# Alternating the matmuls of two accumulators in a hybrid gMLP and pooling layer

## The chip, the core and the metric

The kernel runs on one core of one Trainium2 chip. A core has a matrix engine (TensorE, PE in the profile; its weight loads are PEld), a vector engine (VectorE, DVE), a scalar engine (ScalarE, ACT), GpSimd (POOL) and SyncE (SP), which issues most of the DMAs here. The engines run side by side, each through its own list of instructions in order, and wait for each other by semaphores. The metric is the device time of one execution in microseconds, the median of several runs.

## The reference

One layer of a streaming encoder is computed for 4096 new rows of a prompt and 32 rows of a sample stream, with model width 1024, all in float32:

- h = RMSNorm(x); one projection h @ w_in gives five parts of 1024 columns: u, v, z_a, x_b, z_b.
- Branch A: v is layer-normed; per head (8 heads of 128 columns) a masked 128x128 matrix mixes the 128 positions of a chunk; a = u * (mixed v + bias) * silu(z_a).
- Branch B: trailing means of x_b over 2, 4, 8 or 16 rows minus x_b itself, a linear map for each of four groups, a scale; b = that * silu(z_b).
- y = x + concat(a, b) @ w_out, then a final RMSNorm. Also returned are the last 15 rows of x_b for both streams and the normed v rows of the sample.

## The kernel before

*Products.* Every large matrix product is done in two ways at once. It is cut 2 x 2 and computed with seven block products instead of eight (the Strassen scheme in Winograd's form): operand sums are made beforehand, the seven products are numbered q = 0 to 6, and their results are added up. And each float32 operand is split into a high and a low part that TensorE takes in one pass each (type float32r); a product of two operands is high x high, high x low and low x high. So one block product over four slices k of 128 is twelve matmuls (lines 186 to 194, `product`): for each k the pairs (stationary, moving) are (high, high), (high, low), (low, high). All twelve add into one accumulator, a PSUM bank of 128 x 512 float32. TensorE is told at the first of them to overwrite, where the accumulator is a fresh one.

*Accumulators.* `Combine` (lines 146 to 179) names the accumulators of one output block and what happens behind each product. Products 0, 1, 3 and 5 begin a fresh bank. Products 2 and 4 go on adding to the bank of product 0, product 6 to that of product 3. Behind product 0, ScalarE copies bank 0 into y11 (line 167); behind product 1, VectorE adds bank 1 to y11 (line 165); behind product 2, ScalarE copies bank 0 again into y21 (line 172); behind product 4 it copies it into y12 (line 174) and VectorE adds bank 3 to make y22; behind 5 and 6 VectorE adds banks 5 and 3. So product 2 may not write bank 0 before the copy of line 167 has read it, product 4 not before that of line 172, product 6 not before the sum behind product 4. Six banks serve the pool `ps_acc2`, two more the spatial mixing.

*Stages.* From 0 to about 52 us x_b's and the pool's weights are multiplied together and operands are made; until about 400 us v is projected; from then to 1704 us runs the input projection for the gates, u and the pooling branch, the loop in question; the rest is the output projection (lines 712 to 714) with the final norm.

*The loop in question.* Tokens are four blocks of 1024 rows (b = 0 to 3). In each block there are 16 sets of weight columns: eight of kind gate (z_a and u for one head) and eight of kind pool. The order in a block is a pair of pool sets, eight gate sets one by one, four pool sets one by one, a pair of pool sets; the products of a pair are interleaved by `lagged` (line 181). A set's seven products use 128 weight columns of each half as the stationary operand and 512 token columns as the moving one. The last block also carries the 32 sample rows, so its token half is 528 wide and is worked in two column parts of 264 (`self.groups`), each with its own `Combine` and its own banks. Line 1156 begins a step (s, q): weight operands are prepared LEAD = 5 steps ahead (`prepare`, casts of line 119 on ScalarE and differences of line 81 on VectorE, into seven buffers of the pool `wop_p`); then the products of that step, each followed by its `after`; then, for a gate set, behind q = 2 and q = 4, the spatial mixing of one half (`spatial`, lines 993 to 1002: four float32 matmuls of 128 columns, which the profile shows as eight instructions of line 998, and one VectorE instruction). What finishes a set (silu, products, windows, stores) is traced in the first steps of the next.

*Order.* The program text gives an order of tracing, not the final order. A planner goes through the traced instructions with its own model of times: each engine gets the earliest traced instruction that is ready by that model, and the order found so is fixed in the program. Semaphore waits are then put where an instruction depends on another engine.

Of the kernel before, what the change touches and what calls it, by code (L numbers as in the profile page):

```python
# [36 lines left out]
def stream_step(ctx: ExitStack, tc, x_prompt, x_sample, state_pool, norm_g, w_in, ln_v_g, ln_v_b,  # L37
# [10 lines left out]
    mm = nc.tensor.matmul  # L48
# [15 lines left out]
    part = dram.tile([SEQ + DEC, D], F32, name="part")  # L64
# [121 lines left out]
    def product(comb_, q, stationary, moving, lo_last=False):  # L186

        acc, fresh = comb_.bank(q)
        terms = [(k, s, m) for k in range(4) for s, m in ((0, 0), (0, 1), (1, 0))]
        if lo_last:  # L190
            terms.sort(key=lambda x: x[1])
        for n, (k, s, m) in enumerate(terms):
            mm(acc, stationary(s, k), moving(m, k), start=fresh and n == 0, stop=n == len(terms) - 1,  # L193
               skip_group_check=True)

    def stacked(acc, rows, n, terms):

        last = len(terms) - 1
        for i, (st, wh, wl) in enumerate(terms):
            if i < last:  # L200
                mm(acc[:, :n], st, wh, start=i == 0, stop=False)
            mm(acc[:rows, :n], st[:, :rows], wl, start=False, stop=False)  # L202
        mm(acc[:, :n], st, wh, start=False, stop=True)

    def pool(name, bufs, stack=ctx, **kw):
        return stack.enter_context(tc.tile_pool(name=name, bufs=bufs, reuse_waits="tile", **kw))
# [4 lines left out]
    with ExitStack() as ph:  # L211
# [184 lines left out]
        def comb_rows(i):  # L396
            cols = []
            for q in range(2):
                tr = tr_tile()
                for cc in range(4):  # L400
                    c = 4 * q + cc
                    turn = nc.tensor.transpose(tr[:, cc * P:(cc + 1) * P], rows_t[i][:, c * P:(c + 1) * P], ident)
                    if i == 1 and c == 0:
                        tc.keep_in_program_order(turn)
                cols.append(half())
                (nc.scalar.copy if i > 1 else nc.vector.tensor_copy)(cols[q], tr)
            return cols
# [49 lines left out]
        class Pair:  # L457
# [72 lines left out]
            def product(self, q):  # L530
                t = self.ops[q].rearrange("p h (k t) -> p h k t", t=P)
                product(self.c, q, lambda h, k: t[:, h, k, :], lambda h, k: wv[q][:, h, k, :])
                self.c.after(q)
# [20 lines left out]
        parts = comb_rows(0)  # L554
        for i in range(KT):
# [8 lines left out]
            parts = nxt  # L564
# [56 lines left out]
    def raw_tile(dt=F32):  # L621
        return raw_p.tile([P, D], dt, tag="raw", name="raw")
# [9 lines left out]
    def load_out_weights(z, q):  # L632
        w_slots[z, q] = t = slot()[:, :4 * D].rearrange("p (k h n) -> p k h n", k=4, h=2)
        nc.sync.dma_start(t.bitcast(F32), wops[z, q].rearrange("p k (h n) -> p k h n", h=2))
# [229 lines left out]
    with ExitStack() as ph:  # L864
# [50 lines left out]
        class Tokens:  # L915
# [17 lines left out]
            def moving(self, q, h, k, c0, n):  # L933
                if self.last:
                    return self.ops[q].rearrange("p (h k t) -> p h k t", h=2, t=WIDE)[:, h, k, c0:c0 + n]
                return self.ops[q][:, :8 * HALF].rearrange("p (h j k t) -> p h k j t", h=2, j=4, t=P)[:, h, k]

        class Set:
# [40 lines left out]
            def combine(self, c0, n):  # L979
                def first(y):  # L980
                    if self.kind == "gate":
# [2 lines left out]
                return Combine(n, acc_tile, first,  # L984
                               *[lambda y=y: self.result(y, c0, n) for y in ("11", "12", "21", "22")])

            def product(self, c, q, c0, n):
                t = self.ops[q]
                product(c, q, lambda h, k: t[:, h, k, :], lambda h, k: self.tok.moving(q, h, k, c0, n),
                        self is groups[0][0] and q == 0)  # L990
                c.after(q)
# [117 lines left out]
        def prepare(upto):  # L1109

            nonlocal done
            while done < min(upto, len(steps)):
                while loads and loads[0][0] <= done + (AHEAD if done < first[id(groups[n_sets][0])] + 7 else 6):
                    loads.pop(0)[2].load()
                s, q = steps[done]
                s.prep[q]()
                if done in beside:
                    w, q = beside[done]
                    w.prep[q]()
                done += 1  # L1120
# [25 lines left out]
        for n in range(n_sets):  # L1146
            g, order = groups[n], orders[n]
            for s in g:
                s.begin()
            if n == n_sets - 5:  # L1150
                w_stack.close()
                spare_p = pool("spare_p", 2, side="right")
            elif n == n_sets - 1:
                groups[n_sets][0].begin([spare_p.tile([P, D], F32, tag="spare", name="spare") for _ in range(2)], True)
            cs = {id(s): [(s.combine(c0, w), c0, w) for c0, w in s.tok.groups] for s in g}
            for s, q in order:
                at += 1
                prepare(at + LEAD)
                while later:
                    (later.pop(0) or (lambda: None))()  # L1160
                for c, c0, w in cs[id(s)]:
                    s.product(c, q, c0, w)
                if n == 0 and q == 0:
                    behind.append(s)
                if s is g[-1] and groups[n + 1][0].stage != s.stage:
                    if n + 1 < n_sets:
                        groups[n + 1][0].tok.load(q)
                    else:
                        if q == 3:
                            groups[n_sets][1].begin([raw_tile(), raw_tile()], True)  # L1170
                        load_out_weights(0, q)
                if n == 0 and s is g[-1] and q in (3, 5):
                    next(constants, None)
                if s.kind == "gate" and q in (2, 4):
                    if q == 2:
                        s.t1 = []
                    s.t1.append(s.spatial(len(s.t1)))
                if s.kind == "gate" and q == 6 and s.tok.last:
                    s.spatial_sample()
                if q == NQ - 1:  # L1180
                    later.append(s.finish_gate() if s.kind == "gate" else s.finish_pool())
# [4 lines left out]
    with ExitStack() as ph:  # L1186
# [56 lines left out]
        for n in range(n_sets, len(groups)):  # L1243
            g, order = groups[n], orders[n]
# [5 lines left out]
            for m, (s, q) in enumerate(order):  # L1250
# [4 lines left out]
                k = n - n_sets - 4  # L1255
# [48 lines left out]
```

## Time and profile before

| | |
|---|---|
| time, median of three runs | 2348.82 us (2346.55 to 2349.65) |
| the profiled execution, from its first to its last instruction | 2345.9 us |
| TensorE busy | 2328.8 us, 99% |
| weight loads on TensorE busy | 1981.3 us, 84% |
| VectorE, ScalarE, GpSimd busy | 1790.2, 896.4, 215.1 us |
| matmuls of line 193 on prepared weights, 512 columns | 4032 |
| matmuls of line 193 on prepared weights, 264 columns | 2688 |

The profile shows one execution; apart from its span no other time of it is given. In the groups a row gives the source line, engine, operation, what is written and read, the count, the busy time and mean length of one, then the idle time of the engine in front of them and what ended it. Consecutive matmuls overlap in the records, so the length of one is more than the distance from its start to the next one's. The chain of waits lists pieces of unbroken work in order of time: start, length, engine, tile, line, count. The timeline lists instructions of an engine, merged where they follow each other: start, length from the first's start to the last's end, engine, line, operation, shapes, count, and in brackets the idle time before and who ended it.

### The profile page before, as it was taken

To read this page: it belongs to the slowest core of one execution; us is meant where nothing else is said; L and a number is where in the kernel's file an instruction comes from. 1 tells how busy PE (TensorE), PEld (TensorE's weight loads), DVE (VectorE), ACT (ScalarE), POOL (GpSimd) and SP (SyncE) were. 2 spreads that over 40 slices of the span, in tenths; PEclk is the share of its full clock that TensorE was granted. 3 is DMA by queue.
4 is the path that set the end of the run, shared out by engine and by line. 5 is a ranking of instruction groups with operands and counts; after the bars stand their busy time and mean duration, and the time that the engine had idled before them with its cause. 6 is when DMAs were issued, how large, how long until landed. Compare 5 with 4: busy or idle time off the path is not lost.

```text
span 2345.9 us, 32604 instructions
## 1 busy us (share of the span) xinstructions
PE 2328.8 (99%) x11936; PEld 1981.3 (84%) x11936; DVE 1790.2 (76%) x3318; ACT 896.4 (38%) x1603; POOL 215.1 (9%) x398
## 2 busy tenths in 40 slices
PE   8999999999999999999999999999999999999998
PEld 7878888888888888888888899999987878888877
DVE  7877786866787767877668876668777778688887
ACT  6545544433433333433334333334322333233333
POOL 1010000100021000111000110102200000000000
PEclk9999999999999999999999999999999999999999
DMA  8879977432448334483334472335587776955542
GB/s 309 316 241 279 275 255 245 142 104 89 149 144 296 99 100 134 135 300 122 108 108 148 177 262 87 101 100 164 223 294 265 252 257 232 360 171 169 159 137 90
DMA packets 325145, 445.69 MB, mean 190 GB/s; under 512 B 19324, under 2 KB 248444, under 8 KB 322296
## 3 DMA queue, kind: packets, MB, share of 16 engines
q1 hardware_dynamic: 273384, 355.05, 45.9%
q0 software_dynamic: 22288, 73.48, 8.3%
q10 hardware_dynamic: 29312, 15.08, 2.4%
q8 instruction: 94, 1.54, 0.3%
q14 instruction: 67, 0.55, 0.1%
HBM read 273.88 MB, written 169.66 MB: 189 GB/s over the span
## 4 chain that ended last, share of the span: by engine, by line
PE 95%; DMA 2%; DVE 2%; issue 0%; ACT 0%; SPq 0%; ACTq 0%; DVEq 0%
PE acc L193 66%; PE acc L712 8%; PE acc L713 8%; PE acc L714 8%; PE sp L998 2%; PE tr L473 1%; DMA wops<-raw 1%; DMA vt<-in_w_in_dram 1%; PE acc L261 0%; DMA op<-in_w_in_dram 0%; PE more L844 0%; PE more L843 0%; DVE wop L81 0%; DVE y L724 0%; PE acc L202 0%
## 5 line engine op out<-in xcount | busy, mean ns | idle before, releaser
L193 PE MATMUL acc<-slot,wop 128*128 128x512 f32 (+1 forms) x6720 | 1260.9, 348 | 1.0 <-DVE wop L81 1.0
L193 PEld LDWEIGHTS acc<-slot,wop 128*128 128x128 f32 x6720 | 1081.1, 188 | 156.5 <-DVE wop L81 1.4
L81 DVE TENSOR_TENSOR wop<-raw,wop 128x512 fp32r<-128x512 f32 (+1 forms) x510 | 353.4, 695 | 133.0 <-ACT wop L119 121.7
L119 ACT CAST wop<-raw 128x512 fp32r<-128x512 f32 x340 | 210.5, 622 | 384.4 <-PE acc L193 266.9
L712 PE MATMUL acc<-slot,wop 128*128 128x512 f32 x892 | 347.2, 389 | 1.5 <-DVE y L724 1.5
L713 PE MATMUL acc<-slot,wop 128*128 128x512 f32 x892 | 347.1, 389 | 0.0
L714 PE MATMUL acc<-slot,wop 128*128 128x512 f32 x892 | 347.0, 389 | 0.0
L193 PE MATMUL acc<-slot,op 128*128 128x512 f32 x1344 | 323.8, 395 | 0.3 <-ACT vt L167 0.2
L193 PEld LDWEIGHTS acc<-slot,op 128*128 128x128 f32 x1344 | 247.6, 188 | 51.9 <-ACT vt L167 0.7
L165 DVE TENSOR_TENSOR t<-acc,t 128x512 f32<-128x512 f32 (+1 forms) x320 | 186.7, 584 | 120.0 <-ACT t L174 65.5
L724 DVE TENSOR_TENSOR y<-acc,y 128x512 f32<-128x512 f32 x235 | 159.3, 687 | 72.6 <-PE acc L714 72.2
L712 PEld LDWEIGHTS acc<-slot,wop 128*128 128x128 f32 x892 | 167.4, 188 | 37.8 <-ACT wop L677 2.3
L714 PEld LDWEIGHTS acc<-slot,wop 128*128 128x128 f32 x892 | 167.4, 188 | 34.8
L713 PEld LDWEIGHTS acc<-slot,wop 128*128 128x128 f32 x892 | 167.4, 188 | 34.7
L677 ACT CAST wop<-raw 128x512 fp32r<-128x512 f32 x160 | 98.7, 622 | 175.2 <-PE acc L714 164.9
L81 DVE TENSOR_TENSOR wop<-sum,wop 128x512 fp32r<-128x512 f32 x200 | 136.9, 685 | 25.7 <-ACT wop L119 24.9
L1017 POOL DMA_DIRECT2D abT<-t x128 | 69.2, 541 | 843.2 <-DVE t L1029 622.7
L119 ACT CAST wop<-sum 128x512 fp32r<-128x512 f32 x136 | 84.5, 622 | 96.9 <-PE acc L193 72.0
L1040 DVE TENSOR_TENSOR t<-t 128x527 f32<-128x527 f32 (+3 forms) x160 | 111.1, 698 | 0.6
L677 ACT CAST wop<-sum 128x512 fp32r<-128x512 f32 x64 | 39.7, 622 | 119.5 <-PE acc L714 96.3
L174 ACT COPY t<-acc 128x512 f32<-128x512 f32 (+1 forms) x80 | 40.2, 504 | 107.1 <-PE acc L193 105.4
L115 DVE TENSOR_TENSOR sum<-raw 128x512 f32<-128x512 f32 x68 | 46.8, 688 | 44.7 <-DMA raw<-in_w_in_dram 44.1
(236 smaller groups left out, 1955.0 us busy)
## 6 DMA issues: line engine op xcount, KB each, us to landing
raw<-in_w_in_dram SPq DMA_DIRECT2D x102, 512.0 KB, 4.3
xops<-op SPq DMA_DIRECT2D x72, 512.0 KB, 6.1
abT<-t POOLq DMA_DIRECT2D x128, 256.0 KB, 3.8
raw<-abT SPq DMA_DIRECT2D x64, 512.0 KB, 5.0
slot<-xops SPq DMA_DIRECT2D x30, 1024.0 KB, 9.6
slot<-wops SPq DMA_DIRECT2D x14, 2048.0 KB, 9.7
xt<-in_x_prompt_dram SPq DMA_DIRECT2D x32, 512.0 KB, 5.0
raw<-v_all SPq DMA_DIRECT2D x32, 512.0 KB, 3.3
```

What stands on the lines that cost most here:

```text
L81: return nc.vector.tensor_tensor(out, src, hi.bitcast(F32), ALU.subtract)
L119: pair = nc.scalar.copy(hi, src), lo_part(lo, src, hi)
L165: add = lambda o, x, y: nc.vector.tensor_tensor(o, x, y, ALU.add)
L193: mm(acc, stationary(s, k), moving(m, k), start=fresh and n == 0, stop=n == len(terms) - 1, skip_group_check=True)
L677: nc.scalar.copy(t[:, 0], src)
L712: mm(acc, x[:, 0, k, :], w[:, k, 0, c], start=fresh and k == 0, stop=False, skip_group_check=True)
L713: mm(acc, x[:, 0, k, :], w[:, k, 1, c], start=False, stop=False, skip_group_check=True)
L714: mm(acc, x[:, 1, k, :], w[:, k, 0, c], start=False, stop=k == 3, skip_group_check=True)
L724: nc.vector.tensor_tensor(y, self.acc[bank], y, ALU.add)
L998: mm(sp[:, a, :], self.v[:, 4 * hf + a, :], WT[:, h, :], start=True, stop=True)
L1017: nc.gpsimd.dma_start(abT[row, :, t0:t0 + HALF], t[:, :HALF])
L1040: tt(nxt[:, lo:HALO + m], s[:, lo:HALO + m], s[:, lo - step:HALO + m - step], ALU.add)
```

## The change

A new function `products` takes several parts, each an accumulator with its two operands, and issues their matmuls in turn: first term of the first part, first term of the second, second term of the first, and so on. It is used in two places of the loop over steps.

- In the last block, the two column parts of one product alternate (24 matmuls, two accumulators; for pairs of sets too, product by product). Both `after`s follow behind the 24.
- In the first three blocks, for the sets that go one by one, product 0 is not issued in its own step; in the step of product 1 the matmuls of products 0 and 1 alternate (24 matmuls, two accumulators, with different stationary and moving operands). Both `after`s follow behind them. The steps keep their preparation and what else they trace; products 2 to 6 are as before, and so are the pairs.

```diff
+    def products(parts):
+        parts = [(*comb_.bank(q), stationary, moving) for comb_, q, stationary, moving in parts]
+        terms = [(k, s, m) for k in range(4) for s, m in ((0, 0), (0, 1), (1, 0))]
+        for n, (k, s, m) in enumerate(terms):
+            for acc, fresh, stationary, moving in parts:
+                mm(acc, stationary(s, k), moving(m, k), start=fresh and n == 0, stop=n == len(terms) - 1,
+                   skip_group_check=True)
...
+            def part(self, c, q, c0, n):
+                t = self.ops[q]
+                return c, q, lambda h, k: t[:, h, k, :], lambda h, k: self.tok.moving(q, h, k, c0, n)
...
-                for c, c0, w in cs[id(s)]:
-                    s.product(c, q, c0, w)
+                if s.tok.last:
+                    products([s.part(c, q, c0, w) for c, c0, w in cs[id(s)]])
+                    for c, c0, w in cs[id(s)]:
+                        c.after(q)
+                elif len(g) == 1 and q < 2:
+                    (c, c0, w), = cs[id(s)]
+                    if q == 0:
+                        both = [s.part(c, 0, c0, w)]
+                    else:
+                        products(both + [s.part(c, 1, c0, w)])
+                        c.after(0)
+                        c.after(1)
+                else:
+                    for c, c0, w in cs[id(s)]:
+                        s.product(c, q, c0, w)
```

## The prediction

> **What bounds the kernel now.** I read the page's head first, then the groups of TensorE by shape, then the busy time by stretches (blocks 0 to 2 of the input projection, the last block, the output stage).
>
> ```profile
> span 2345.9 us, 32604 instructions
> ...
> PE 2328.8 (99%) x11936; PEld 1981.3 (84%) x11936; DVE 1790.2 (76%) x3318; ACT 896.4 (38%) x1603; POOL 215.1 (9%) x398
> ```
> ```profile
> L193 PE MATMUL acc<-slot,wop 128*128 128x512 f32 x4032 | 928.1, 390 | 1.0 <-DVE wop L81 1.0
> ...
> L193 PE MATMUL acc<-slot,wop 128*128 128x264 f32 x2688 | 332.9, 285 | 0.0
> ```
> ```profile
> core 0: us, PE busy (x) PEld busy (x) DVE busy (x) ACT busy (x) POOL busy (x), PEclk, DMA share, GB/s
> 1340.00:1700.00 360.00, 360.00 (x2883) 355.09 (x2882) 263.79 (x507) 130.55 (x266) 54.47 (x111) 1.00 0.47 163
> 440.00:1320.00 880.00, 880.00 (x4075) 735.33 (x4074) 660.94 (x1049) 320.16 (x549) 94.62 (x148) 1.00 0.44 143
> ```
>
> TensorE is busy for the whole of both stretches that the change touches, at full granted clock (1.00), and its idle time in front of 6720 matmuls of line 193 comes to 1.0 us. So there is no stall to remove. The time can only change if a matmul takes another slice of the stream, or if the new order makes a stall. Each matmul has a weight load (11936 of each), although of every three matmuls two in a row use the same stationary operand; the change leaves both numbers as they are.
>
> The mean duration of a group (390 ns) is the length of one pipelined matmul, not its price. The price is read from the chain of waits, as pieces of unbroken matmuls:
>
> ```profile
> 601.11 165.98 PE acc L193 x732
> ...
> 829.65 0.89 PE sp L998 x8
> 830.54 5.46 PE acc L193 x24
> 836.00 0.89 PE sp L998 x8
> 836.89 13.62 PE acc L193 x60
> ```
> ```profile
> 1415.45 0.89 PE sp L998 x8
> 1416.34 5.83 PE acc L193 x48
> 1422.17 0.33 PE sp L1009 x2
> 1422.50 8.94 PE acc L193 x72
> ...
> 1581.58 122.82 PE acc L193 x1008
> ```
>
> With 512 columns a matmul costs 165.98/732 = 0.2267 us, with 264 columns 5.83/48 = 0.1215 us. The pieces also show a set's rhythm: a gate set in blocks 0 to 2 runs products 5, 6, 0, 1, 2 as 60 matmuls, eight instructions of spatial mixing, products 3 and 4 as 24, eight more.
>
> **Part 1, the pace under alternation.** Touched are 36 single sets (12 in each of three blocks) with 24 matmuls of 512 columns each, 864 of the 4032, and all 2688 of the last block. From the two prices, (226.7 - 121.5)/(512 - 264) = 0.424 ns a column, which leaves 226.7 - 512 x 0.424 = 9.5 ns a matmul that does not go with the columns. If waiting for one's own accumulator were that remainder, alternation could take it away: 3552 x 9.5 ns = 34 us, the bound on the side of a gain. The bound on the other side comes from the one place where two accumulators already take turns, two matmuls each, in the rows of line 1220:
>
> ```profile
> 1825.83 0.23 PE acc L714
> 1826.06 0.23 PE more L1220
> 1826.29 0.24 PE more L1221
> 1826.52 0.23 PE more L1220
> 1826.75 0.23 PE more L1221
> 1826.98 0.23 PE acc L712
> ```
>
> From 1826.06 to 1826.98 are four matmuls at 0.23 us, against 0.2267 in a long run: no faster, at most 3.3 ns dearer each (the output height changes there too), so 3552 x 3.3 ns = 12 us is the bound for a loss. The nearest rows are the long runs themselves: the 732 matmuls hold 60 changes of accumulator, one every twelve, and the 1008 of the last block 83, and neither is cheaper per matmul than the 24s and 48s. I take 0.
>
> The Trainium skill (TensorE: Matmul & The Clock Gate, section Back-to-back issue gap) gives a warm gap of N/2.4 + 2.5 ns whatever is accumulated, 215.8 ns for 512 columns and 112.5 for 264; the trace is 10.9 and 9.0 ns dearer, and if alternation brought it down to the page's figures, an estimate of 864 x 10.9 + 2688 x 9.0 ns = 34 us would be saved. The page names no cost of staying on one bank, and this trace has none at a change.
>
> **Part 2, the copy that loses its cover.** In the 36 single sets product 0 used to end, product 1 ran for 12 x 0.2267 = 2.72 us, and behind it ScalarE's copy (line 167) emptied accumulator 0, which product 2 then writes again. Now product 0 ends one matmul before product 1. The copy is priced here:
>
> ```profile
> 836.65 13.86 PE L193 MATMUL acc<-slot,wop 128*128 128x512 f32 x60
> ```
> ```profile
> 842.43 0.62 ACT L119 CAST wop<-raw 128x512 fp32r<-128x512 f32 x1 [2.08 <-DVE t L1029]
> 843.11 0.63 ACT L1027 ACTIVATE t<-t 128x512 f32<-128x512 f32 x1
> 845.10 0.59 ACT L167 COPY t<-acc 128x512 f32<-128x512 f32 x1 [1.36 <-PE acc L193]
> ```
>
> Product 0 is the third dozen of these 60. Its last matmul starts 35 gaps after 836.65; a gap is (13.86 - 0.39)/59 = 0.228, so at 844.64. The copy ends at 845.69, 1.05 us later. In the changed order product 2 could start two gaps, 0.45 us, after that last matmul, so it would wait 0.60 us with ScalarE free. With a cast of 0.62 us just begun it waits 1.22. What is queued behind it on TensorE is everything, if the order is kept as written: 36 x 0.60 to 36 x 1.22 = 22 to 44 us.
>
> But the order on each engine is made by the planner, which puts a later instruction first when the earlier one is not ready by its own reckoning. The trace shows it doing exactly that at this wait:
>
> ```profile
> 442.98 0.58 ACT L167 COPY t<-acc 128x512 f32<-128x512 f32 x1
> ```
> ```profile
> 444.93 0.38 PE L998 MATMUL sp<-WT,raw 128*128 128x128 f32 x2
> 445.07 3.02 PE L193 MATMUL acc<-slot,wop 128*128 128x512 f32 x12
> 447.93 0.83 PE L998 MATMUL sp<-WT,raw 128*128 128x128 f32 x6
> 448.51 5.74 PE L193 MATMUL acc<-slot,wop 128*128 128x512 f32 x24
> ```
>
> In the code all eight instructions of spatial mixing stand behind product 2. Here two of them run ahead of its twelve. The copy that product 2 needs had ended at 443.56, 1.5 us before the product ran, so the planner reckoned the copy later than the chip had it. That errs on the safe side. In the 24 gate sets the cover is the eight spatial instructions, 0.89 us in the rows above; in the 12 pool sets it is product 3, whose accumulator is a fresh one, three matmuls = 0.68 us. Both exceed 0.60, neither reaches 1.22. Without the cover the price is the 22 to 44 us. I take 0.4 us for what is left open, nearest to the row, where nothing waited.
>
> Moving spatial instructions has a price of its own when they are split: the piece behind eight of them, 24 matmuls in 5.46, holds the change of kind.
>
> ```profile
> 830.30 5.70 PE L193 MATMUL acc<-slot,wop 128*128 128x512 f32 x24
> ```
>
> Its 23 gaps take 5.70 - 0.39 = 5.31 us, against 23 x 0.2267 = 5.21: 0.1 us for each change back. 0 to 24 x 0.1 = 2.4 us; half, 1.2.
>
> Held back along with product 0 are its weights, in one of seven operand buffers, for 2.72 us longer. ScalarE's next cast into that buffer serves the seventh product on, more than five products of 2.72 us = 13.6 us later, which covers it. VectorE's sum into y11 waits for accumulator 1, which ends when it did. No DMA moves: the loads are issued where they were.
>
> **Part 3, the last block.** Both column parts of a product now end together, so the first part's copies and sums start 12 x 0.1215 = 1.46 us later, and the lead to the product that reuses the accumulator falls from 36 matmuls (4.4 us) to 24 (2.9 us).
>
> ```profile
> 1424.25 0.38 ACT L167 COPY t<-acc 128x264 f32<-128x264 f32 x1 [0.83 <-PE acc L193]
> 1425.66 0.38 ACT L167 COPY t<-acc 128x264 f32<-128x264 f32 x1 [1.03 <-PE acc L193]
> ```
> ```profile
> L165 DVE TENSOR_TENSOR t<-acc,t x130: 418/432/692, 1343.7 to 1699.9; 128x264 f32<-128x264 f32 x124, 128x512 f32<-128x512 f32 x6
> ...
>   PEld acc L193: 0.2, 1
> ```
>
> Two copies (0.76) and two sums (0.86) make 1.62 us, inside the 2.9. VectorE is busy for 264 of the 360 us, so queueing adds to it, and TensorE waited for such a sum once, for 0.2 us, in the whole block. Cost 0, with 16 sets x 0.7 = 11 us if in each set a queued sum of 0.69 came in front and nothing covered it.
>
> **The sum.** 2345.9 (profiled span) + 0 + 0.4 + 1.2 + 0 = 2347.5 us. The three runs lie 0.7 to 3.8 above that span, their median 2.9; that difference is carried along: 2350.4, rounded 2350.
>
> **The rivals.** *Slower: the two accumulators end together and the copy stands in the open.* The point from which it decides is a copy that ends later than the cover that the planner put in: 0.89 us in a gate set, 0.68 in a pool set. For it: ScalarE casts 0.62 us at a time, in strict order, and an unlucky copy ends 1.22 us late. Against it: the rows at 444.93, and ScalarE's 320 busy of 880 us. Wholly uncovered it gives 2349 + 22 to 44 = 2371 to 2393; half covered 2360 to 2371. The Trainium skill (Perfetto Trace Analysis, section Matmuls) wants independent groups in different banks so that emptying one runs under the next one's matmuls; this change rotates the banks but ends the two groups together, and by that rule the rival is right. The trace agrees that the copy now runs under product 1; whether spatial work takes over that part no run here shows yet.
>
> *Faster: the 9.5 ns was a wait on one's own accumulator.* It gives 2349 - 34 = 2315, in part perhaps 2340. For it: a fixed remainder exists. Against it: the pieces with an accumulator change every dozen, and the rows of line 1220.
>
> *Slower in the last block:* sums queued on VectorE hold product 6, 11 us, 2360. For it the one wait of 0.2 us; against it a lead of 2.9 us.
>
> *Nothing alternates:* if product 1's operands are late in the planner's reckoning, it runs product 0 straight through, and the time is the old 2349. The casts run five products ahead, so I expect this nowhere.
>
> **How the numbers follow.** A measurement of this kernel can tell 0.2%, 4.7 us, from no change. Forecast (covered, with or without real alternation): 0.67, nearly all of it within 4.7 us. The open copy, in part or whole: 0.16. The last block's sums: 0.05. Faster pace: 0.10. The 0.02 left are the forecast's own spread, half to each side. So faster 0.11, same 0.67, slower 0.22. The range runs from 2343, below which lies most of the faster case, to 2367, which takes in the half-covered copy and the last block; outside are about 0.08 and 0.10.
>
> **What would show it.** Right: pieces of long runs still at 0.2267 and 0.1215 us a matmul; in gate sets of blocks 0 to 2 the piece of 60 becomes 48, then spatial instructions, then twelve; idle time in front of the matmuls of the set loop under 3 us. Wrong: idle of 0.3 us or more put down to ScalarE's copy at some 36 places, or pieces with another price per matmul.

## The result, and the profile after

The changed kernel takes 2355.78 us (median of five runs, 2354.89 to 2358.22), the kernel before beside it on the same chip 2348.31 (2346.55 to 2349.65). The ratio is 1.0035 with a 95% interval of 1.0021 to 1.0048: the change costs about 7.5 us. The forecast was 2350, no measurable change.

The page's head after the change, and TensorE's groups by shape (columns as before):

```profile
span 2356.4 us, 32604 instructions
...
PE 2337.2 (99%) x11936; PEld 1984.1 (84%) x11936; DVE 1790.2 (76%) x3318; ACT 889.3 (38%) x1603; POOL 227.9 (10%) x398
```
```profile
L193 PE MATMUL acc<-slot,wop 128*128 128x512 f32 x3168 | 743.3, 393 | 0.9 <-DVE wop L81 0.9
...
L202 PE MATMUL acc<-slot,wop 128*128 128x264 f32 x2688 | 335.4, 286 | 0.0
```

The numbers of instructions are the same, TensorE is still at 99%, and no new idle time has appeared in front of the matmuls of the loop. The matmuls that alternate now stand under line 202. Spatial mixing has moved from line 998 to 1011. The busy time in the stretch of the first three blocks:

```profile
440.00:1320.00 880.00, 880.00 (x4052) 732.01 (x4052) 657.17 (x1040) 314.77 (x544) 100.97 (x148) 1.00 0.43 143
```

TensorE is busy for all 880 us at full clock, as before, but gets through 4052 matmuls instead of 4075. The 23 that are missing are worth 23 x 880/4075 = 5.0 us. So the loss is not in listed idle time, and it is not in the granted clock (1.00 in both): matmuls take a longer slice of the stream. The chain of waits shows which (a gate set of the second block; the piece at 845.05 is products 0 and 1 alternating):

```profile
839.60 5.46 PE acc L193 x24
845.05 5.44 PE acc L202 x24
850.49 0.67 PE sp L1011 x6
851.16 2.87 PE acc L193 x12
854.02 0.22 PE sp L1011 x2
854.25 5.49 PE acc L193 x24
859.74 0.89 PE sp L1011 x8
```

Compare the rows of before that the prediction shows: 60 matmuls in 13.62, eight spatial instructions, 24 in 5.46, eight more. The 24 alternating matmuls take 5.44 us, 0.2267 each: the old price exactly. Six of the eight spatial instructions stand in front of product 2 and two behind it; before, the planner had split them once, two and six. Product 2 is dear: 2.87 us for twelve where 12 x 0.2267 = 2.72 would do, and the 24 behind the other two take 5.49 instead of 5.46. The set takes 0.18 us longer.

For the experiments I read one more thing from the trace: the start of each single matmul, and from it how long a stage lasts, from the start of its first matmul to the start of the next stage's first (the last block: to the start of its own last). This leaves out what differs between executions outside the loop. That matters here, because the profiled execution after the change is the slowest of its five, and the output stage differed by up to 4 us between executions of kernels that leave it alone. In microseconds, in brackets the difference to the kernel before (the last block of the kernel before holds one wait of a weight load for VectorE's sum, 0.19 us at 1600.71, which the four kernels at -0.2 do not have; the set with it takes 20.76 us, and 20.51 in those):

```
                                  ratio (95% interval)     blocks 0 to 2     last block
before                                                     961.96            345.08
after                             1.0035 (1.0021-1.0048)   967.08 (+5.1)     347.61 (+2.5)
last block alone                  1.0013 (1.0004-1.0022)   961.99 ( 0.0)     347.30 (+2.2)
first three blocks alone          1.0029 (1.0018-1.0041)   966.98 (+5.0)     344.84 (-0.2)
product 1, then 0, then 2         1.0032 (1.0019-1.0044)   969.47 (+7.5)     344.84 (-0.2)
spatial halves together           0.9999 (0.9990-1.0008)   961.55 (-0.4)     345.19 (+0.1)
last block, operands alternate    1.0004 (0.9995-1.0013)   962.00 ( 0.0)     346.07 (+1.0)
last block, accumulators altern.  1.0005 (0.9996-1.0014)   962.00 ( 0.0)     346.32 (+1.2)
last block, only single sets      1.0009 (1.0000-1.0017)   961.95 ( 0.0)     346.48 (+1.4)
alternating, 3 in front of 2      1.0018 (1.0009-1.0026)   964.72 (+2.8)     345.18 (+0.1)
alternating, 8 spatial before 2   1.0002 (0.9993-1.0010)   963.16 (+1.2)     344.84 (-0.2)
that, in the gate sets alone      1.0001 (0.9992-1.0010)   961.91 ( 0.0)     344.84 (-0.2)
```

### The profile page after: what moved, and what is told of

The parts are those of the page before. It is cut to its first block, busy times and chain, and to the rows that moved or that the text cites. A ratio compares the mean times of both kernels' runs of the same rounds, so it can differ in the third digit from the quotient of the medians.

```text
span 2356.4 us, 32604 instructions
## 1 busy us (share of the span) xinstructions
PE 2337.2 (99%) x11936; PEld 1984.1 (84%) x11936; DVE 1790.2 (76%) x3318; ACT 889.3 (38%) x1603; POOL 227.9 (10%) x398
## 4 chain that ended last, share of the span: by engine, by line
PE 87%; issue 8%; DMA 2%; DVE 1%; POOL 1%; ACT 0%; SPq 0%; POOLq 0%; ACTq 0%; DVEq 0%
PE acc L193 44%; PE acc L202 22%; PE acc L721 6%; PE acc L722 6%; PE acc L723 6%; PE sp L1011 2%; PE tr L482 1%; DMA vt<-in_w_in_dram 1%; DMA wops<-raw 0%; POOL part L744 0%; DMA op<-in_w_in_dram 0%; DMA part<-y 0%; PE acc L211 0%; PE more L853 0%; DVE wop L81 0%
## 5 line engine op out<-in xcount | busy, mean ns | idle before, releaser
L193 PE MATMUL acc<-slot,wop 128*128 128x512 f32 x3168 | 743.3, 393 | 0.9 <-DVE wop L81 0.9
L202 PE MATMUL acc<-slot,wop 128*128 128x264 f32 (+1 forms) x3552 | 537.5, 311 | 0.0
L721 PE MATMUL acc<-slot,wop 128*128 128x512 f32 x892 | 347.7, 390 | 3.3 <-DVE y L733 3.2
L722 PE MATMUL acc<-slot,wop 128*128 128x512 f32 x892 | 347.3, 389 | 0.0
L723 PE MATMUL acc<-slot,wop 128*128 128x512 f32 x892 | 347.3, 389 | 0.0
L165 DVE TENSOR_TENSOR t<-acc,t 128x512 f32<-128x512 f32 (+1 forms) x320 | 181.7, 583 | 140.1 <-ACT t L174 72.7
L119 ACT CAST wop<-sum 128x512 fp32r<-128x512 f32 x136 | 84.7, 624 | 90.7 <-PE acc L193 47.6
```

The costliest lines, as they stand in the source:

```text
L119: pair = nc.scalar.copy(hi, src), lo_part(lo, src, hi)
L165: add = lambda o, x, y: nc.vector.tensor_tensor(o, x, y, ALU.add)
L721: mm(acc, x[:, 0, k, :], w[:, k, 0, c], start=fresh and k == 0, stop=False, skip_group_check=True)
L722: mm(acc, x[:, 0, k, :], w[:, k, 1, c], start=False, stop=False, skip_group_check=True)
L723: mm(acc, x[:, 1, k, :], w[:, k, 0, c], start=False, stop=k == 3, skip_group_check=True)
```

## The experiments

**The two halves of the change.** Each half by itself; the edits against the changed kernel:

```diff
# last block alone
-                elif len(g) == 1 and q < 2:
+                elif False:
# first three blocks alone
-                if s.tok.last:
+                if False:
-                elif len(g) == 1 and q < 2:
+                elif len(g) == 1 and not s.tok.last and q < 2:
```

> Only the last block alternates; the first three blocks are as before. In the trace of the change the last block took 347.6 us, before 345.1. Theory A (the loss there is made in the last block itself: 0.5 ns more per alternating matmul, 1.4 us, and about 1 us of waits in its two pairs of sets): the last block again 347.4 to 347.8, the first three at 323.6, 319.2 and 319.2, the time 2.5 us above before. Theory B (any new order of the program costs about as much, by the way the planner lays it out): the first three blocks lose too.

> Only the first three blocks alternate products 0 and 1; the last block is as before. Theory A (the open copy: product 2 waits for ScalarE's copy of accumulator 0 behind six of the eight spatial instructions, and the two left over cost a second change between float32 and float32r matmuls): a gate set 21.0 us against 20.85, a single pool set 19.1 to 19.2 against 19.04, the three blocks 5.1 us longer together, the last block 345.1, the time 5 us above before. Theory B (alternating matmuls are dearer by themselves): the 24 alternating matmuls of a set take more than 24 x 226.7 ns.

Measured: 2350.51 us for the last block alone and 2354.21 for the first three, against 2347.56 of before. The losses are +2.2 us in the last block and +5.0 in the first three, together 7.2 of the 7.6 that the two stages lose with the whole change. The next runs take the two apart.

**What makes product 2 dear.** The rows of the same gate set, first TensorE's timeline after the change, then ScalarE's:

```profile
844.89 5.60 PE L202 MATMUL acc<-slot,wop 128*128 128x512 f32 x24
850.33 0.83 PE L1011 MATMUL sp<-WT,raw 128*128 128x128 f32 x6
851.00 3.03 PE L193 MATMUL acc<-slot,wop 128*128 128x512 f32 x12
853.86 0.38 PE L1011 MATMUL sp<-WT,raw 128*128 128x128 f32 x2
854.00 5.74 PE L193 MATMUL acc<-slot,wop 128*128 128x512 f32 x24
```
```profile
850.36 0.58 ACT L167 COPY t<-acc 128x512 f32<-128x512 f32 x1 [3.91 <-PE acc L202]
```

The last matmul of product 0 starts at 849.88 (the one before the last of the 24). The copy ends at 850.94, 1.06 us later, and product 2 starts at 851.00, 0.06 behind the copy. In single starts: the sixth spatial instruction holds the stream 110 ns, where the last one before the change held it about 30; so 80 ns were spent waiting for the copy, which no view shows as idle time. It is so in 17 of the 24 gate sets; in the other seven the wait is 25 ns. In all 24 product 2 starts 52 or 53 ns behind the copy's end, so it waits for the copy each time. Then the first matmul of product 2 takes 334 ns (314 before), the eleven that follow 225 to 236, most of them 228 and more, where before they are back at 226 or 227 after three.

These late matmuls are not the wait's doing alone. The prediction shows the one gate set of the kernel before that the planner had split: twelve matmuls in 3.02 at 445.07, 24 in 5.74 at 448.51. The copy had ended 1.5 us earlier, and the last spatial instruction held the stream 30 ns both times, so nothing waited; yet the rows are as long as here, 3.03 and 5.74 (24 behind eight are 5.70). From start to start that set takes 20.94 us, where the others take 20.85, and where the spatial halves stand together (a run below) it takes 20.84. So splitting the eight into two and six costs 0.09 us by itself. Of what a gate set loses here, 0.11 to 0.18 us, 0.09 goes to the split and the rest, 0.02 to 0.09, to the wait.

Is it the nearness of the copy, or the alternation, or the split of the spatial instructions? The first test takes the alternation away and keeps the nearness: product 1 runs first, whole, then product 0, then product 2. Against the kernel with the first three blocks alone:

```diff
-                        products(both + [s.part(c, 1, c0, w)])
+                        products([s.part(c, 1, c0, w)])
+                        products(both)
```

> No matmul alternates: in the first three blocks product 1 runs first, as twelve matmuls in a row, then product 0, then product 2, so accumulator 0 is copied in the open as in the change, and a little more so (its last matmul is the very last one). In this program all eight spatial instructions stand together between product 0 and product 2 in gate sets. Theory A (open copy plus split): gate sets have no second change, 20.85 to 20.95; pool sets, which have only product 3 to put in between, 19.1 to 19.2 as in the change; the three blocks 1 to 3 us longer together. Theory B (alternation itself): no loss at all, 0.

Measured: ratio 1.0032, +7.5 us in the first three blocks, above both expectations. In the chain of waits a gate set reads:

```profile
843.85 5.44 PE acc L202 x24
849.29 0.89 PE sp L1011 x8
850.18 8.26 PE acc L193 x36
```

The timelines of the two engines at that product 2:

```profile
849.13 1.05 PE L1011 MATMUL sp<-WT,raw 128*128 128x128 f32 x8
849.96 6.21 PE L193 MATMUL acc<-slot,wop 128*128 128x512 f32 x26
```
```profile
849.32 0.59 ACT L167 COPY t<-acc 128x512 f32<-128x512 f32 x1 [2.05 <-PE acc L202]
```

Nothing alternates and all eight spatial instructions stay together, in front of product 2; yet the 36 matmuls behind them take 8.26 us where 36 x 0.2267 = 8.16, and a gate set loses 0.09 us. Product 2 starts here at 849.96, again 0.05 us behind its copy's end at 849.91. In 20 of the 24 gate sets the wait is only 29 ns (in four 84), and the late matmuls behind it do the rest. So neither alternation nor the split is needed for a loss of 0.09 us: a short wait for the copy makes it alone. Most of the rest of the 7.5 us is another matter, two waits of 1.8 us, one in the second block and one in the third (their two sets lose 4.4 us together), shown by TensorE's timeline and, below it, ScalarE's:

```profile
959.48 2.79 PE L193 MATMUL acc<-slot,wop 128*128 128x512 f32 x11 [1.80 <-ACT t L172]
```
```profile
958.32 0.62 ACT L119 CAST wop<-raw 128x512 fp32r<-128x512 f32 x1 [5.04 <-DMA wops<-wop]
958.85 0.58 ACT L172 COPY t<-acc 128x512 f32<-128x512 f32 x1
```

The copy of line 172 stood behind a cast that waited 5.04 us for a DMA. In the kernel before, ScalarE's timeline has them the other way round at this place:

```profile
953.45 0.59 ACT L172 COPY t<-acc 128x512 f32<-128x512 f32 x1 [2.55 <-PE acc L193]
953.93 0.62 ACT L119 CAST wop<-raw 128x512 fp32r<-128x512 f32 x1
956.81 0.62 ACT L119 CAST wop<-sum 128x512 fp32r<-128x512 f32 x1 [2.26 <-DMA wops<-wop]
```

The order came with the new plan, and I did not foresee it.

**The price of changing between spatial mixing and products.** The prediction charged 0.1 us for each change back. The kernel before, with both spatial halves behind product 4, has half as many changes:

```diff
-                if s.kind == "gate" and q in (2, 4):
-                    if q == 2:
-                        s.t1 = []
-                    s.t1.append(s.spatial(len(s.t1)))
-                if s.kind == "gate" and q == 6 and s.tok.last:
-                    s.spatial_sample()
+                if s.kind == "gate" and q == 4:
+                    s.t1 = [s.spatial(hf) for hf in range(2)]
+                    if s.tok.last:
+                        s.spatial_sample()
```

> The kernel before, with both halves of the spatial mixing (and in the last block the sample's) behind product 4 instead of one half behind product 2 and one behind product 4. If each change from float32 to float32r matmuls costs 0.09 us, as the split in the change suggests, one change fewer in each of 32 gate sets saves 2.9 us: a gate set of the first three blocks 20.76 instead of 20.85; in the last block the sample's two changes (0.17 us a set) go as well, 1.4 us; the time 3 to 4.5 us below before. If the 0.09 us is not a cost of the change, the time is that of before.

```profile
836.09 19.05 PE acc L193 x84
855.14 1.78 PE sp L998 x16
856.93 19.05 PE acc L193 x84
```

A set now takes 19.05 + 1.78 = 20.83 us. Before it was 13.62 + 0.89 + 5.46 + 0.89 = 20.86, and from set to set by single starts 20.84 against 20.85. So a change is worth about 0.01 us. The single starts say why: the first matmul behind spatial mixing takes 314 ns instead of 227, but it starts 30 ns after the last spatial instruction instead of 111. What it holds on to longer, it has begun earlier. This holds behind eight spatial instructions and behind sixteen, where the eleven matmuls after the first lose 9 ns together. Behind two or six, with no wait, they lose 46 ns in every trace that has such a place, and that is the price of the split above. (In the last block of this kernel a weight load of the sample's spatial work waits 0.2 us for VectorE eight times, which may be why that block is 0.1 us longer.)

**The last block.** Alternating does two things there: consecutive matmuls switch between two accumulators, and they switch between two moving operands. One kernel does each by itself (against the kernel with the last block alone; the terms are the 24 matmuls in their order). Both leave out that each term belongs to the accumulator of its own column part:

```diff
# operands alternate, accumulators straight
+                    terms = [(k, a, m, p) for k in range(4) for a, m in ((0, 0), (0, 1), (1, 0)) for p in ops]
+                    for i, (c, c0, w) in enumerate(cs[id(s)]):
+                        acc, fresh = c.bank(q)
+                        for j, (k, a, m, p) in enumerate(terms[12 * i:12 * i + 12]):
+                            mm(acc, p[2](a, k), p[3](m, k), start=fresh and j == 0, stop=j == 11,
...
# accumulators alternate, operands straight
+                    terms = [(k, a, m, p) for p in ops for k in range(4) for a, m in ((0, 0), (0, 1), (1, 0))]
...
+                    for j, (k, a, m, p) in enumerate(terms):
+                        acc, fresh = banks[j % 2]
+                        mm(acc, p[2](a, k), p[3](m, k), start=fresh and j < 2, stop=j > 21, skip_group_check=True)
```

> On the kernel before, in the last block alone: the 24 matmuls of a product read their operands in the changed order (first term of the first column part, first term of the second, and so on), but the first twelve add into the first accumulator and the last twelve into the second, each emptied as before. (So sums are put together wrongly: this leaves the assignment of terms to column parts out, and keeps every instruction, size and wait.) In the changed kernel an undisturbed 264-column matmul of the last block took 122.0 ns from start to start, before 121.5. Theory A (the half nanosecond comes from the order in which the operands are read): 121.9 to 122.1 here, no extra waits, the last block 1.2 to 1.5 us longer. Theory B (it comes from changing accumulators at each matmul): 121.5, and the last block as before, 345.1 us.

> The other half: in the last block alone the operands are read in the old order (twelve terms of the first column part, then twelve of the second), but the matmuls add into the two accumulators by turns, and both are emptied behind the 24. (The assignment of terms to column parts is again left out.) Theory A (order of operands): 121.5 ns a matmul, and only the waits in the two pairs of sets, about 1 us in the last block. Theory B (changing accumulators): 122.0 ns and 1 us of waits, together 2.2 to 2.5 us, as in the changed kernel.

The same 48 matmuls between two spatial halves, in the chain of waits after the change, with operands alternating, and with accumulators alternating (5.83 before):

```profile
1416.02 5.87 PE acc L202 x48
```
```profile
1416.11 5.85 PE acc L1180 x48
```
```profile
1416.11 5.83 PE acc L1180 x48
```

Taken over all 264-column matmuls that nothing disturbs, the distance from start to start is 121.46 ns before, 122.02 after, 121.91 with operands alternating, 121.52 with accumulators alternating. So the change of accumulator is free at the matmuls themselves (0.06 ns). The changed order of operands costs 0.45 ns a matmul, 2688 x 0.45 = 1.2 us; the +1.0 measured is that less the 0.2 us wait that the kernel before has and this one has not. With the moving operands in turn, the stationary ones change places too (four matmuls in a row on the high part and two on the low one, before two and one), so which of the two orders costs it is not shown. The accumulators' part lies elsewhere. The waits of TensorE's weight loads in the last block (who waits for whom: total us, times, longest), after the change and with accumulators alternating:

```profile
PEld acc L202 <- ACT t L174: 0.4, 2, 0.2
PEld acc L202 <- DVE t L165: 0.2, 1, 0.2
```
```profile
PEld acc L1180 <- ACT t L174: 0.4, 2, 0.2
PEld acc L1180 <- DVE t L165: 0.2, 1, 0.2
```

Where only operands alternate no such wait is left. By single starts the dear sets are those of the pairs: 20.7 us in the first pair and up to 21.04 in the last where accumulators alternate, against 20.39 before. The listed waits are 0.6 us of it. The two losses add up, 1.0 + 1.2 = 2.2 us, to what the last block alone had lost; measured from a straight block without the 0.2 us wait (344.84) they are 1.2 + 1.5 = 2.7 against 2.5, so the agreement is no better than 0.2. A last kernel confines the alternation in this block to the sets that go one by one:

```diff
-                if s.tok.last:
+                if s.tok.last and len(g) == 1:
```

> Only the last block alternates, and there only the twelve sets that go one by one; its two pairs run straight as before. Theory A (of the 2.2 us that alternation in the last block costs, the pairs make 1 us by waits for accumulators and the pace makes the rest): the first and last two sets of the block back to 20.39 each, gate sets still 22.80 against 22.73, pool sets 20.44 against 20.39; the last block 345.9 to 346.2 us. Rival (the pairs cost nothing): 347.3 as with all sets.

Measured: the pairs are back at 20.39 us a set and no weight load waits, but the last block takes 346.48, above the 346.2 expected. The twelve single sets are dearer than they were: a gate set takes 22.86 us and a pool set 20.49 to 20.65, where with the last block alone it was 22.80 and 20.44 to 20.55, and the 264-column matmuls stand 122.05 ns apart instead of 121.91. At 0.45 ns for 2016 matmuls 0.9 us would be left, less the 0.2 us wait; +1.4 are. So what the order of operands costs differs from kernel to kernel (in the full change it is 122.02), and why stays open.

**More distance between products 0 and 2.** Three kernels give product 2 more time, with the alternation in the first three blocks kept and straight products in the last block. In the first, product 3 goes ahead of product 2, and both spatial halves stand behind product 2 (in the last block all spatial work behind product 4):

```diff
+                elif len(g) == 1 and not s.tok.last and q in (2, 3):
+                    for c, c0, w in cs[id(s)]:
+                        s.product(c, 5 - q, c0, w)
...
-                if s.kind == "gate" and q in (2, 4):
...
+                if s.kind == "gate" and q == (4 if s.tok.last else 3):
+                    s.t1 = [s.spatial(hf) for hf in range(2)]
...
```

> First three blocks: products 0 and 1 alternate as in the change, but then product 3 (a fresh accumulator) runs ahead of product 2, and both spatial halves stand between product 2 and product 4, so that every copy of accumulator 0 has at least 1.7 us of other work in front of the product that writes it next. Last block straight as before, its spatial work together behind product 4. Theory A (the loss of the first blocks is the copy in the open): gate sets 20.84 us, as in the kernel with spatial work together and no alternation, the three blocks within 0.5 us of before except for pool sets, where product 4 now waits for the copy behind product 2 (0 to 0.15 us each); the time within 1.5 us of before. Theory B (alternation costs by itself, or the tighter order does): gate sets 21.0 still, the time 4 us or more above before.

The weight loads' waits and the matmuls' own in the first three blocks:

```profile
PEld acc L193 <- ACT t L172: 4.3, 13, 1.1
```
```profile
PE acc L193 <- ACT t L172: 0.9, 2, 0.7
```

Gate sets are at 20.84 us, as with the spatial halves together and nothing alternating; only the first of all has a wait and takes 21.09. In the pool sets, which have no spatial mixing to stand between products 2 and 4, the loss has moved one product on: product 4 now follows product 2 at once and its weight load waits for the copy of line 172, at the other 12 of the 13 places. +2.8 us remain, more than the 1.5 expected; 1.9 of it lies in one pool set of each block, which loses 0.44 to 1.01 us.

The second is the smaller step. The first spatial half is traced behind product 1 instead of product 2, so that eight of its instructions, not six, stand in front of product 2: 0.22 us more. The last kernel does this and alternates in the gate sets alone. Against the first three blocks alone:

```diff
-                if s.kind == "gate" and q in (2, 4):
-                    if q == 2:
+                if s.kind == "gate" and q in ((2, 4) if s.tok.last else (1, 4)):
+                    if q < 4:
# and, for the gate sets alone
-                elif len(g) == 1 and not s.tok.last and q < 2:
+                elif len(g) == 1 and not s.tok.last and s.kind == "gate" and q < 2:
```

> First three blocks alternate; in their gate sets the first half of spatial mixing is traced ahead of product 2, so all eight of its instructions (0.89 us) stand between products 1 and 2, not six (0.67 us). Theory A (product 2 begins just as the copy of bank 0 ends, and its first matmuls then run without a lead of their weight loads): by the start of product 0's last matmul the copy ends 1.05 us later, and product 2 may now begin 0.45 + 0.89 = 1.34 us later, so it has 0.29 us to spare. A gate set takes 20.84 to 20.88 us (21.02 with six), and the loop is 1 to 2 us longer than before (the twelve pool sets' share), where it was 5.0. Rival B (the split of eight into six and two is what costs): the same 20.84 here, but then the run with product 1 ahead of product 0, which kept the eight together and lost 0.09 us a set, is not explained. Rival C (any start of product 2 within some 3 us of product 0's end is slow, however long the copy is done): a gate set stays at 20.93 or above, and the loop at +3 us or more.

> As the run above, but the pool sets of the first three blocks are straight as before: only the 24 gate sets alternate, with eight spatial instructions as cover. Theory A: loop within 0.8 us of before, no waits of product 2 on the copy; the ratio's interval holds 1. Rival C: loop +2 us (24 x 0.09) or more. If alternation by itself saved anything, this kernel would show it: a loop shorter than before by more than 0.5 us.

The chain of waits of a gate set with eight ahead, and the two engines' timelines at its product 2:

```profile
841.45 5.44 PE acc L202 x24
846.89 0.89 PE sp L1011 x8
847.78 8.18 PE acc L193 x36
```
```profile
846.73 1.05 PE L1011 MATMUL sp<-WT,raw 128*128 128x128 f32 x8
847.53 8.42 PE L193 MATMUL acc<-slot,wop 128*128 128x512 f32 x36
```
```profile
846.75 0.59 ACT L167 COPY t<-acc 128x512 f32<-128x512 f32 x1 [3.91 <-PE acc L202]
```

The copy ends at 847.34, and product 2 starts at 847.53, 0.19 us later. The 36 matmuls take 8.18 us, where with product 1 ahead of product 0 they took 8.26, and a gate set 20.85 us, the time of before. The lead expected was 0.29 and is 0.19, mostly because the last spatial instruction again holds the stream only 30 ns. This takes away the wait and the split at once, so it does not tell their shares; the set that was split without a wait and the run with product 1 first do. What remains, +1.2 us, is in the single pool sets, which have no spatial instructions; there the weight load of product 2 waits at twelve places, once in each, and starts 0.05 us behind the copy's end every time:

```profile
PEld acc L193 <- ACT t L167: 2.7, 12, 0.3
```

With the gate sets alone this row is gone too, the first three blocks take 961.91 us against 961.96, and in the stretch from 440 to 1320 us TensorE gets through 4076 matmuls, one more than before:

```profile
440.00:1320.00 880.00, 880.00 (x4076) 735.36 (x4075) 657.97 (x1046) 318.48 (x548) 95.08 (x148) 1.00 0.44 143
```

So 24 sets of 24 matmuls alternate here without loss and without gain. No kernel of these beats the one before; the best stand level with it.

## Why the prediction was right or wrong

The time lay in the range, but the likeliest case, no change that can be measured, did not come. The sum had +1.6 us in it; the two stages lost 7.6. That the range held is luck in part: it was drawn that far for a copy that stands open, which did not come. Point by point:

*Part 1, the pace, taken as 0: right for 512 columns.* 5.44 us for 24 alternating matmuls, and nothing gained or lost in the gate sets that alternate with cover. The 9.5 ns was no wait on one's own accumulator. The gap of 215.8 ns, an estimate by the formula that the Trainium skill gives for a lone matmul on a warm clock (TensorE: Matmul & The Clock Gate, section Back-to-back issue gap), isn't reached with alternating banks either; the trace stays at 226.7. For 264 columns the 0 was wrong by about 0.5 ns a matmul, 1.0 to 1.2 us in the block with operands alternating alone, inside the bounds given (-9.5 to +3.3 ns), and from a side not thought of, the order in which operands are read, not the accumulator.

*Part 2, the copy: the mechanism was right, "0.4 us for what is left open" was mis-sized; it measured 3.1.* The planner covered all 36 copies in part, with spatial instructions or with matmuls of another product. The step that failed is "both exceed 0.60". In a gate set it took 0.89 as the cover, because eight instructions exist, but the planner moved only six (that its own model asked for no more is my guess). Six last 0.59 us where nothing waits, as the last holds the stream for 30 ns: product 2 is ready 0.45 + 0.59 = 1.04 us after product 0's last matmul starts. The copy ends 1.01 or 1.07 us after it (1.05 forecast), and product 2 starts 0.05 behind that end. So it waits 25 or 80 ns, in the 24 gate sets 1.7 us with what follows. In six of the twelve pool sets three matmuls were moved in, the 0.68 us of the forecast, and the copy ended at 1.01. In the other six a cast had begun ahead of the copy, which ended at 1.53, and five matmuls were moved in. Each time product 2's weight load waited. A pool set loses 0.06 to 0.17 us, the twelve 1.4. The step's warning, from the Trainium skill (Perfetto Trace Analysis, section Matmuls), that emptying one group should run under the next one's matmuls, is borne out in small: in a gate set the emptying ran under six spatial instructions, and where eight took their place nothing waited.

*Part 2, the split, "0.1 us for each change back; half, 1.2": near in price, from the wrong row.* The row it was read from has eight instructions ahead, and there a change costs about 0.01 us: the long first matmul was counted without the short slice ahead of it. What costs is the split into six and two, 0.09 us a set by the one set that was split before. The planner split all 24 gate sets, not half of them, so the term measured 2.0 instead of 1.2.

*Part 3, the last block, taken as 0: wrong by 2.5 us of the 11 allowed (2.2 with the last block alone).* Sums and copies do hold three products, in the pairs, where two sets share VectorE and ScalarE, and not in all 16 sets. This is the small form of the rival "slower in the last block". The operands' order, which was not in the forecast, makes about half of it. The three terms together, 3.1 + 2.0 + 2.5, are the 7.6.

*The rivals.* The open copy, fully or half open, did not come (22 to 44 us). A faster pace did not come. That nothing alternates did not come. What came lies between the forecast and the open copy: every copy covered in part, and every cover a little too short. The unlucky copy behind a cast did come, in six pool sets, and five matmuls covered most of it.

*What would show it.* Of the signs named, the idle time stayed under 3 us, as for a right forecast, and idle of 0.3 us at 36 places, the sign of a wrong one, was too coarse. The other sign of a wrong one did come, pieces with another price: 2.87 us for twelve, 5.87 for 48. There is no new idle time in the groups; the loss shows in the length of the pieces and in the count of matmuls in a fixed stretch, and, for the pool sets, in the weight loads' waits.

*What stays open.* Why the restart is slow, behind a wait and behind a split. The lead of the weight loads does not tell the cases apart: the first one starts 28 ns ahead of its matmul both at 445.07, where the matmuls behind are late, and at 851.15 of the same kernel, where it is not, and the next two 230 to 233 ns ahead in both. Why the changed order of operands costs 0.45 to 0.6 ns at 264 columns and nothing at 512 was not tried.

## What to carry to other kernels

When two accumulator groups are made to end together, count for each the time from the start of its last matmul to the reuse of its bank, and subtract the emptying (here 1.06 us). A start 0.05 us behind the copy's end was a wait in this kernel, and cost 0.09 us a set by itself; a start 0.19 us behind it cost nothing; in between nothing was measured for the gate sets. Look also at what is moved in as cover: splitting a group of eight small matmuls cost as much as the longer waits. A planner need not leave a margin, so trace the cover where it is wanted. A busy share of 99% without idle time does not mean that nothing waits: count the instructions in equal stretches, and compare the lengths of like pieces.

## What the runs showed of the hardware

- A wait of 25 to 84 ns on a bank shows as no idle time. The product starts 52 or 53 ns behind the end of the copy that it waits for, in all 24 gate sets after the change.
- Where 512-column matmuls start again behind such a wait, many of the next ten are 228 to 236 ns apart instead of 227. The same happens without a wait behind two or six float32 spatial instructions, 46 ns over eleven matmuls, and not behind eight or sixteen, 9 ns.
- Eight or sixteen float32 spatial instructions in between cost about 0.01 us of change: 314 ns for the next product's first matmul, but about 30 instead of 111 for the spatial one in front of it.
- 264-column matmuls take 121.46 ns apart in the straight order of operands and 121.91 to 122.05 when two moving operands are read in turn; at 512 columns 226.7 either way, and changing the accumulator on every matmul costs nothing at either width.
